# Where a tile is transposed in a two-layer recurrent trunk: matrix engine or vector engine

## The chip, the core and the metric

The kernel runs on one core of a Trainium2 chip. The core has five engines that run their own instruction streams in order: TensorE (PE) multiplies matrices, VectorE (DVE) and ScalarE (ACT) work elementwise, GpSimd (POOL) does a little elementwise work, and SyncE (SP) issues nearly all transfers between HBM and the on-chip memory SBUF. TensorE writes only to PSUM; the other engines read its results from there. The metric is the device time of one execution in microseconds (us), as the median of several runs.

## The reference

A causal decoder trunk of two layers over 512 positions with 2048 channels. Layer 0 joins a gated linear recurrence (RG-LRU) and a matrix LSTM (mLSTM) behind one input projection; layer 1 is a Mamba-2 SSD mixer in 8 groups of 8 heads. Cut to what the change touches:

```
def reference(x, ...):
    x = x + lru_mlstm_layer(rmsnorm(x, e_norm), ...)      # layer 0
    x = x + ssd_layer(rmsnorm(x, o_norm), ...)            # layer 1
    return rmsnorm(x, final_norm)

# layer 0, mLSTM half: per head, v feeds a causal attention with decays
v = einsum('bshi,hij->bshj', xm_h, w_v)
h = mlstm_chunkwise(q, k, v, ig, lf)

# layer 1
z, xbc, dt = split(x @ w_in)
xbc = silu(causal_conv(xbc, conv_w, conv_b))
xs, bm, cm = split(xbc)
da_cs  = cumsum(dt * a)                                   # inside chunks of 128 positions
decay  = exp(where(causal, da_t[l] - da_t[s], -inf))
cb     = einsum('bclgn,bcsgn->bcgls', cm, bm)
y_diag = einsum('bcgls,bcgels,bcsgep->bclgep', cb, decay, xdt)
states = einsum('bclgn,bclge,bclgep->bcgepn', bm, decay_states, xdt)
y      = y_diag + y_off(states) + d_skip * xs
y      = rmsnorm_grouped(y * silu(z)) @ w_out
```

All arrays are float32. Sums over positions (in `y_diag`, `states` and the mLSTM's attention) need `xs`, `bm` and `v` with positions on the partitions, while the projections leave them with channels on the partitions. That is why they are transposed.

## The kernel before

**Tiling.** Activations are tiles of 128 channels by 512 positions. To keep float32 accuracy at the fast matmul format, each operand is split into a high and a low part: `split` (L167 to L169) makes `hi` by a cast on ScalarE and `lo = src - hi` on VectorE. Each product is then three matmuls (`mm3`, L146 to L150: hi·hi, hi·lo, lo·hi). Weights stream from HBM all through the kernel: `load_w` (L129) reads 512 KB into one of two `wraw` buffers by a transfer on SyncE's queue and splits it into two pairs `whi`, `wlo` of 128 x 512, which rotate through four buffers each. `chunk` (L153) uses one such pair for 12 matmuls of 512 columns.

**Order of the work.** A tile framework plans the order of each engine's instructions from the order of the program, with priorities: `load_w` puts its transfer and its splits 3000 instructions ahead, as far as free buffers allow, and `evac` (the step that empties a PSUM bank on VectorE) 1000 ahead. Side work runs in generators: `spawn` starts one, `tick()` is called after nearly every chunk, and `yield n` in a generator means "go on n ticks from now". The table `LAG` (L43) holds these numbers. `tc.issue_after(ins)` orders what is issued inside it behind `ins` on the same engine.

**Layer 0.** For each of 4 heads the kernel projects `xm` and `zm`, then makes 4 tiles of v, 4 of o and 4 of q and k. For each v tile `vgen` (L403) waits 2 ticks, transposes the tile's four 128 x 128 blocks on TensorE into one PSUM bank, copies the bank to `vn` on ScalarE and sends it to HBM (`vd`), from where the attention reads it later.

**Layer 1.** Eight groups follow each other. For each group the kernel projects B and C (`xbc`: projection, evacuation with the norm factor, a causal convolution on ScalarE and VectorE, SiLU on ScalarE), then four tiles `xs` of two heads each, then four gate tiles `z`. Between the second and third tile of either four, some tiles of the previous group's output projection (`outproj`, PSUM tile `po`) are put in; the rest follow at the end. The generator `bcgen` (L748) makes C·B of each chunk (`CB`) and transposes three chunks of B on TensorE (`Btr`), which `split` then reads from PSUM into `Bn`. For each `xs` tile the generator `pair` (L768):

- fetches the two heads' decay sums, broadcast to all partitions (`dab`, two buffers), with a transfer on SyncE's queue;
- after 6 ticks transposes four chunks of `xs` on TensorE into PSUM (`xtr`), and VectorE multiplies that PSUM tile into `xw` (for the states) and `xdt` (for the diagonal part);
- for each head forms `min(dab - dasT, 0)` in four VectorE instructions of 128 x 128 (L798), takes `Exp` on ScalarE (L800) and multiplies by `CB` on VectorE (L801), giving `Pt`;
- after 4 more ticks runs the sixteen small matmuls `yd` and adds their result to `xs`.

The PSUM has three banks for projections (`pmm`) and four for side work (`pax`).

Of the kernel before, what the change touches and what calls it, by code (L numbers as in the profile page):

```python
# [9 lines left out]
F32 = mybir.dt.float32  # L10
F32R = mybir.dt.float32r
AF = mybir.ActivationFunctionType
# [4 lines left out]
P = 128  # L17
# [4 lines left out]
NH = 4  # L22
# [17 lines left out]

NRES = OFF["gsel"][0]

LAG = dict(P=6, rs=2, late=3, dtr=15, CB=5, xtr=6, st=4, sts=2, yo0=4, yo=2, att_rs=4, vtr=2, aitr=12, num=7, pr=2)  # L43

VB = (2, 2)

# [7 lines left out]
def trunk(ctx, tc, x_t, par, w_in0, w_qkvo, w_lru, w_if, w_out0, w_in1, w_out1, out):  # L54
# [68 lines left out]
        while gens:  # L123
            tick()

    last_hi = []


    def load_w(src, dsts=(None, None), ahead=3000):  # L129
        out = []  # L130
        with tc.high_priority(offset=ahead):
            n = src.shape[-1]
            raw = wp.tile([P, 1024], F32, tag="wraw", name="wraw", bufs=2)
            dma(raw[:, :n], src)
            for i in range(0, n, 512):
                m = min(512, n - i)
                if dsts[i // 512] is None:
                    hi = wp.tile([P, 512], F32R, tag="whi", name="whi", bufs=4)
                    lo = wp.tile([P, 512], F32R, tag="wlo", name="wlo", bufs=4)
                else:  # L140
                    hi, lo = dsts[i // 512]
                split(hi[:, :m], lo[:, :m], raw[:, i:i + m])
                out.append((hi, lo))
        return out

# [21 lines left out]
    def split(hi, lo, src):  # L167
        last_hi[:] = [sc.copy(hi, src)]  # L168
        return v.tensor_tensor(lo, src, hi.bitcast(F32), op=SUB)  # L169
# [4 lines left out]
    def axt(name="ax"):  # L174
        return pax.tile([P, S], F32, tag="ax", name=name)


    def recip(dst, src, w=S):
        for o in range(0, w, P):
            v.reciprocal(dst[:, o:o + P], src[:, o:o + P])  # L180

# [183 lines left out]
    for h in range(NH):  # L367
        xm, xc = [], []
        for t in range(4):
            j = 4 * h + t  # L370
            if h:
                ps = mmt("xm")
                proj(ps, w_in0[16 + j], xpairs)
            else:
                ps = ps01[j]
            raw = next_raw()
            evac(raw[:, 3:], ps, r_bc, MUL)
            m = xslot("xm")
            split(m[0], m[1], raw[:, 3:])
            xm.append(m)  # L380
            a = st("ca")
            conv(a, raw, pc("cm_w", 4 * j, 4), pc("cm_b", j))
            sc.activation(a, a, AF.Silu)
            c = xslot("xc")
            split(c[0], c[1], a)
            xc.append(c)
            tick()
            if j == 0:

                softplus(nlam, pc("lam", 0, 16), -1.0, *[st("ln")[:, :16] for _ in range(3)])  # L390
                v.tensor_scalar(nlam, nlam, -8.0, None, op0=MUL)
        zm = []
        for t in range(4):
            j = 4 * h + t
            ps = mmt("zm") if j else axt("zm")
            proj(ps, w_in0[48 + j], xpairs)
            z = PA.tile([P, S], F32, tag="zm", name="zm", bufs=4)
            evac(z, ps, r_bc, MUL)
            sc.activation(z, z, AF.Silu)
            zm.append(z)  # L400
            tick()

        def vgen(vt, h, t):  # L403
            yield LAG["vtr"]
            pt = axt("vtr")
            for s in range(4):
                pe.transpose(pt[:, s * P:(s + 1) * P], vt[:, s * P:(s + 1) * P], ident)
            vn = PA.tile([P, 4, P], F32, tag="vn", name="vn", bufs=2)
            sc.copy(vn.rearrange("p a b -> p (a b)"), pt)
            dma(vd[h][:, :, t * P:(t + 1) * P], vn)  # L410

        def ggen(kt, rhs):
            yield 2
            gate_mm(kt, rhs)

        vts = []
        for t in range(4):
            if t % 2 == 0:
                ws = load_w(w_qkvo[h, 2 + t // 2])
            ps = mmt("v")  # L420
            chunk(ps, ws[t % 2], xm, 0, 4)
            vt = PA.tile([P, S], F32, tag="vt", name="vt", bufs=5)
            sc.copy(vt, ps)
            vts.append(vt)
            spawn(vgen(vt, h, t))
            tick()
        spawn(ggen([16 + 4 * h + t for t in range(4)], vts))
        for t in range(4):
            if t % 2 == 0:
                ws = load_w(w_qkvo[h, 4 + t // 2])  # L430
            ps = mmt("o")
            chunk(ps, ws[t % 2], xm, 0, 4)
            s = st("os")
            sc.activation(s, ps, AF.Sigmoid)
            v.scalar_tensor_tensor(zm[t], zm[t], pc("m_norm", 4 * h + t), s, op0=MUL, op1=MUL)
            dma(od[h][t], zm[t])
            tick()
        qk = []
        for t in range(4):
            if t % 2 == 0:  # L440
                ws = load_w(w_qkvo[h, 0 + t // 2])
            ps = mmt("qk")
            chunk(ps, ws[t % 2], xc, 0, 4)
            q = PA.tile([P, S], F32, tag="qk", name="qk", bufs=4)
            if t < 2:
                sc.copy(q, ps)
                dma(qd[h][t], q)
            else:
                sc.activation(q, ps, AF.Copy, scale=1.0 / 16)
                dma(kd[h][t - 2], q)  # L450
            qk.append(q)
            tick()
        spawn(ggen([2 * h, 2 * h + 1, 8 + 2 * h, 9 + 2 * h], qk))
# [237 lines left out]
    def lt(tag, bufs=1, shape=(P, S), dt=F32):  # L691
        return L1.tile(list(shape), dt, tag=tag, name=tag, bufs=bufs)
# [55 lines left out]
    def bcgen(G):  # L748
        Bt, Ct = G["Bt"], G["Ct"]
        CB = lt("CB", shape=(P, 4, P))  # L750
        Bn = lt("Bnh", shape=(P, 3 * P), dt=F32R), lt("Bnl", shape=(P, 3 * P), dt=F32R)
        G["CB"], G["Bn"] = CB, Bn
        yield LAG["CB"]
        ps = axt("CB")
        for c in range(4):
            cs = slice(c * P, (c + 1) * P)
            pe.matmul(ps[:, cs], Bt[:, cs], Ct[:, cs], start=True, stop=True)
        v.tensor_tensor(CB, ps.rearrange("p (c l) -> p c l", l=P),
                        mask.unsqueeze(1).to_broadcast([P, 4, P]), op=MUL)
        ps = axt("Btr")  # L760
        for c in range(3):
            cs = slice(c * P, (c + 1) * P)
            pe.transpose(ps[:, cs], Bt[:, cs], ident)
        split(Bn[0], Bn[1], ps[:, :3 * P])
        G["bc"] = True


    def pair(G, t, xs):  # L768
        CB = G["CB"]
        j = 4 * G["g"] + t  # L770
        h0 = 2 * j
        pts = []
        dabs = []
        for e in range(2):
            dab = lt("dab", 2)
            dma(dab, dad[h0 + e].partition_broadcast(P))
            dabs.append(dab)
        yield LAG["xtr"]
        assert G["bc"] and len(ready) == 3
        ps = axt("xtr")  # L780
        for c in range(4):
            cs = slice(c * P, (c + 1) * P)
            pe.transpose(ps[:, cs], xs[:, cs], ident)
        p4 = ps.rearrange("p (c h d) -> p c h d", h=2, d=64)
        xdt = lt("xdt", 2, (P, 4, P))
        if t == 0:
            G["xw"] = lt("xw", 1, (P, 3, 4, P))
        xw = G["xw"][:, :, t].rearrange("p c (h d) -> p c h d", d=64)
        v.tensor_tensor(xw, p4[:, 0:3],
                        dwT[:, 0:3, h0:h0 + 2].unsqueeze(3).to_broadcast([P, 3, 2, 64]), op=MUL)  # L790
        v.tensor_tensor(xdt.rearrange("p c (h d) -> p c h d", d=64), p4,
                        dtT[:, :, h0:h0 + 2].unsqueeze(3).to_broadcast([P, 4, 2, 64]), op=MUL)
        if t == 3:
            spawn(states(G))
        for e in range(2):
            pt = lt("Pt", 2, (P, 4, P))
            for c in range(4):
                v.tensor_scalar(pt[:, c], dabs[e][:, c * P:(c + 1) * P], dasT[:, c, h0 + e:h0 + e + 1], 0.0,  # L798
                                op0=SUB, op1=MIN)
            sc.activation(pt, pt, AF.Exp)  # L800
            v.tensor_tensor(pt, pt, CB, op=MUL)  # L801
            pts.append(pt)
        yield LAG["st"]
        pd = axt("yd")
        for c in range(4):
            for e in range(2):
                pe.matmul(pd[e * 64:(e + 1) * 64, c * P:(c + 1) * P], xdt[:, c, e * 64:(e + 1) * 64],
                          pts[e][:, c], start=True, stop=True)
        v.scalar_tensor_tensor(xs, xs, pc("dskip", j), pd, op0=MUL, op1=ADD)
        G["yd"][t] = xs  # L810
# [332 lines left out]
```

## Time and profile before

| | |
|---|---|
| median of 3 runs | 2628.41 us (2628.21 to 2628.78) |
| the profiled execution, its own time | 2627.02 us |
| its span, first to last instruction | 2625.2 us |
| VectorE busy | 1670.0 us, 64% |
| ScalarE busy | 1214.5 us, 46% |
| transfers | 295 MB, 33.8% of the 16 DMA engines' time |

In the profile a line of a timeline gives start and duration in us, the engine (PE for a matmul, PEld for the weight load before it), the line of the code, the operation, `out<-in` by tile names, the shape and the count, and in brackets the idle time before it with what ended that. Matmuls overlap in their pipeline: the listed duration of one is its latency, and what it costs the stream is the distance from one start to the next. A row of `lines` gives a group's busy time and the mean duration of one; a row of `windows` the busy time (and the number of instructions) of PE, weight loads, VectorE, ScalarE and GpSimd in a stretch of time.

### The profile page before, as it was taken

The numbers are of one execution on the slowest core, as the hardware profiler recorded it, in microseconds if no ns is written. First come the engines' busy times: TensorE is split into PE (matmuls) and PEld (weight loads), VectorE is DVE, ScalarE is ACT, GpSimd is POOL, SyncE is SP. The second block draws the span as 40 slices with busy tenths as digits, with TensorE's granted clock in tenths as the row PEclk, the third lists the DMA queues.
The fourth block names the chain that finished last, engine by engine and source line by source line (L and its number), as shares of the span: only waits on it lengthen the run. The fifth ranks groups of instructions, "written<-read, shape, count | busy, mean of one in ns | idle before, by whom it ended". The sixth has DMA issues, their size and how long they took to land. (4 is left out here: it accounts for less than half of the span.)

```text
span 2625.2 us, 32843 instructions
## 1 busy us (share of the span) xinstructions
PE 2610.6 (99%) x12289; PEld 2149.0 (82%) x12289; DVE 1670.0 (64%) x2746; ACT 1214.5 (46%) x1895; POOL 118.2 (5%) x107
## 2 busy tenths in 40 slices
PE   9999999999999999999999999999999999999998
PEld 8887878788888888888888888888888888888887
DVE  8452534488757757765777666666666666666675
ACT  6443443476536446453554333443434434334444
POOL 1000000010000000000200000000000000000002
PEclk9999999999999999999999999999999999999999
DMA  5424242533333333332253332333333333233322
GB/s 185 135 98 144 93 141 96 159 105 129 115 107 112 115 103 104 106 109 97 87 130 109 104 117 97 115 105 105 108 104 113 102 104 117 93 118 107 105 98 105
DMA packets 113919, 295.09 MB, mean 112 GB/s; under 512 B 11992, under 2 KB 37336, under 8 KB 113760
## 3 DMA queue, kind: packets, MB, share of 16 engines
q1 hardware_dynamic: 113616, 292.73, 33.8%
q8 instruction: 97, 1.59, 0.2%
q14 instruction: 62, 0.51, 0.1%
q10 hardware_dynamic: 144, 0.26, 0.0%
HBM read 275.89 MB, written 17.06 MB: 112 GB/s over the span
## 5 line engine op out<-in xcount | busy, mean ns | idle before, releaser
L168 ACT CAST whi<-wraw 128x512 fp32r<-128x512 f32 (+1 forms) x881 | 541.3, 615 | 1026.4 <-PE po L149 276.0
L169 DVE TENSOR_TENSOR wlo<-wraw,whi 128x512 fp32r<-128x512 f32 (+1 forms) x881 | 622.9, 708 | 510.3 <-ACT whi L168 484.4
L148 PE MATMUL xbc<-xh,whi 128*128 128x512 f32 x768 | 301.1, 392 | 0.0
L150 PE MATMUL xbc<-xh,wlo 128*128 128x512 f32 x768 | 299.0, 389 | 0.0
L149 PE MATMUL xbc<-xl,whi 128*128 128x512 f32 x768 | 298.9, 389 | 0.0
L227 DVE TENSOR_TENSOR acc<-acc,po 128x512 f32<-128x512 f32 (+1 forms) x257 | 174.2, 680 | 178.7 <-PE po L150 178.2
L148 PE MATMUL z<-xh,whi 128*128 128x512 f32 x512 | 203.9, 398 | 0.0
L150 PE MATMUL z<-xh,wlo 128*128 128x512 f32 x512 | 199.8, 390 | 0.0
L149 PE MATMUL z<-xl,whi 128*128 128x512 f32 x512 | 199.3, 389 | 0.0
L148 PE MATMUL po<-yh,whi 128*128 128x512 f32 (+1 forms) x456 | 178.1, 390 | 0.0
L150 PE MATMUL po<-yh,wlo 128*128 128x512 f32 (+1 forms) x456 | 176.8, 388 | 0.0
L149 PE MATMUL po<-yl,whi 128*128 128x512 f32 (+1 forms) x456 | 176.6, 387 | 0.0
L148 PEld LDWEIGHTS xbc<-xh,whi 128*128 128x128 f32 x768 | 144.2, 188 | 30.5 <-issue 1.2
L150 PEld LDWEIGHTS xbc<-xh,wlo 128*128 128x128 f32 x768 | 144.1, 188 | 30.3
L149 PEld LDWEIGHTS xbc<-xl,whi 128*128 128x128 f32 x768 | 144.2, 188 | 29.4
L245 POOL TENSOR_TENSOR ssq<-ssq,sq 128x512 f32<-128x512 f32 x51 | 66.3, 1300 | 1571.4 <-ACT sq L244 1571.4
L150 PEld LDWEIGHTS z<-xh,wlo 128*128 128x128 f32 x512 | 96.1, 188 | 20.9
L149 PEld LDWEIGHTS z<-xl,whi 128*128 128x128 f32 x512 | 96.3, 188 | 18.8
L148 PEld LDWEIGHTS z<-xh,whi 128*128 128x128 f32 x512 | 96.2, 188 | 18.5
L148 PE MATMUL zl<-xh,whi 128*128 128x512 f32 x256 | 101.4, 396 | 0.0
L148 PE MATMUL po<-ylh,whi 128*128 128x512 f32 x256 | 100.7, 393 | 0.0
L150 PEld LDWEIGHTS po<-yh,wlo 128*128 128x128 f32 x456 | 85.6, 188 | 17.9
(372 smaller groups left out, 5311.2 us busy)
## 6 DMA issues: line engine op xcount, KB each, us to landing
wraw<-in_w_in_dram SPq DMA_DIRECT2D x287, 512.0 KB, 3.2
wraw<-in_w_out_dram SPq DMA_DIRECT2D x128, 512.0 KB, 3.2
dab<-dad SPq DMA_DIRECT2D x64, 256.0 KB, 3.2
wraw<-in_w_qkvo_dram SPq DMA_DIRECT2D x24, 512.0 KB, 3.2
E<-ed SPq DMA_DIRECT2D x64, 96.0 KB, 2.7
vd<-vn SPq DMA_DIRECT2D x16, 256.0 KB, 3.7
od<-zm SPq DMA_DIRECT2D x16, 256.0 KB, 3.8
V<-vd SPq DMA_DIRECT2D x16, 256.0 KB, 3.9
```

Of the source, the lines that this page charges most:

```text
L148: pe.matmul(ps, wh, mh, start=first, stop=False)
L149: pe.matmul(ps, wh, ml, start=False, stop=False)
L150: return pe.matmul(ps, wl, mh, start=False, stop=last)
L168: last_hi[:] = [sc.copy(hi, src)]
L169: return v.tensor_tensor(lo, src, hi.bitcast(F32), op=SUB)
L227: v.tensor_tensor(o, a, b, op=op)
L245: eng.tensor_tensor(ssq, ssq, sq, op=ADD)
```

## The change

- `flip` is new. It transposes on VectorE: for a tile of 128 partitions it issues, for each of four source quadrants `a` and four target quadrants `b`, one instruction that transposes the 32 x 32 blocks of `n` chunks, 16 instructions in all for a whole tile. Each reads 32 partitions by `n` x 32 elements from SBUF and writes as many to SBUF. All are ordered behind the last `lo` instruction of a weight split traced so far, which `last_lo` remembers.
- `vgen`: all v tiles but the last of the last head are flipped into `vn` in four parts of four instructions, one tick apart, starting after 2 + 3t ticks for tile t. The last one is done as before.
- `bcgen`: in groups 1 to 7, B is flipped into an SBUF tile from the `s` ring in two parts of eight instructions, one tick apart (`n` is 3), and split from there.
- `pair`: in groups 1 to 7, `xs` is flipped into `xdt` in two parts of eight instructions (`n` is 4) at ticks 4 and 5. At tick 6, as before, `xw` and then `xdt` itself, in place, are made from that tile in SBUF. Group 0 is transposed on TensorE as before.
- `min(dab - dasT, 0)` becomes `relu(dasT - dab)` on ScalarE, in as many instructions, in all eight groups, and the sign moves into the `Exp`.

```diff
-LAG = dict(P=6, ..., CB=5, xtr=6, st=4, ...)
+LAG = dict(P=6, ..., CB=5, flip=4, xtr=2, st=4, ...)

-                split(hi[:, :m], lo[:, :m], raw[:, i:i + m])
+                last_lo[:] = [split(hi[:, :m], lo[:, :m], raw[:, i:i + m])]

+    def flip(dst, src, lo, hi):
+        n = dst.shape[1]
+        s4 = src[:, :n * P].rearrange("p (c b i) -> p c b i", b=4, i=32)
+
+        with tc.issue_after(last_lo[0].ins):
+            for a in range(lo, hi):
+                pa = slice(32 * a, 32 * a + 32)
+                for b in range(4):
+                    v.transpose(dst[32 * b:32 * b + 32, :, pa], s4[pa, :, b])

         def vgen(vt, h, t):
-            yield LAG["vtr"]
-            pt = axt("vtr")
...
+            if h == NH - 1 and t == 3:
+                yield LAG["vtr"]
+                pt = axt("vtr")
...
+            else:
+
+                yield LAG["vtr"] + 3 * t
+                vn = PA.tile([P, 4, P], F32, tag="vn", name="vn", bufs=2)
+                for a in range(4):
+                    if a:
+                        yield 1
+                    flip(vn, vt, a, a + 1)
             dma(vd[h][:, :, t * P:(t + 1) * P], vn)

+        if G["g"] == 0:
...
+        else:
+            bt = st("bt")[:, :3 * P].rearrange("p (c n) -> p c n", n=P)
+            flip(bt, Bt, 0, 2)
+            yield 1
+            flip(bt, Bt, 2, 4)
+            split(Bn[0], Bn[1], bt.rearrange("p c n -> p (c n)"))

-        yield LAG["xtr"]
+        yield LAG["flip"]
+        xdt = lt("xdt", 2, (P, 4, P))
+        if G["g"]:
+            flip(xdt, xs, 0, 2)
+            yield LAG["xtr"] - 1
+            flip(xdt, xs, 2, 4)
+            yield 1
+            p4 = xdt.rearrange("p c (h d) -> p c h d", d=64)
+        else:
+
+            yield LAG["xtr"]
+            ps = axt("xtr")
...
             for c in range(4):
-                v.tensor_scalar(pt[:, c], dabs[e][:, c * P:(c + 1) * P], dasT[:, c, h0 + e:h0 + e + 1], 0.0,
-                                op0=SUB, op1=MIN)
-            sc.activation(pt, pt, AF.Exp)
+                sc.activation(pt[:, c], dabs[e][:, c * P:(c + 1) * P], AF.Relu, bias=dasT[:, c, h0 + e:h0 + e + 1],
+                              scale=-1.0)
+            sc.activation(pt, pt, AF.Exp, scale=-1.0)
```

More of the change, by code (lines that the diff above doesn't have):

```diff
@@ L41 @@
 NRES = OFF["gsel"][0]
-LAG = dict(P=6, rs=2, late=3, dtr=15, CB=5, xtr=6, st=4, sts=2, yo0=4, yo=2, att_rs=4, vtr=2, aitr=12, num=7, pr=2)
+LAG = dict(P=6, rs=2, late=3, dtr=15, CB=5, flip=4, xtr=2, st=4, sts=2, yo0=4, yo=2, att_rs=4, vtr=2, aitr=12, num=7, pr=2)
 VB = (2, 2)
@@ L124, in drain @@
             tick()
-    last_hi = []
+    last_hi, last_lo = [], []
     def load_w(src, dsts=(None, None), ahead=3000):
@@ L403, in vgen @@
         def vgen(vt, h, t):
-            yield LAG["vtr"]
-            pt = axt("vtr")
[L406 to L409, printed above, removed]
+            if h == NH - 1 and t == 3:
+                yield LAG["vtr"]
+                pt = axt("vtr")
+                for s in range(4):
+                    pe.transpose(pt[:, s * P:(s + 1) * P], vt[:, s * P:(s + 1) * P], ident)
+                vn = PA.tile([P, 4, P], F32, tag="vn", name="vn", bufs=2)
+                sc.copy(vn.rearrange("p a b -> p (a b)"), pt)
+            else:
+                yield LAG["vtr"] + 3 * t
+                vn = PA.tile([P, 4, P], F32, tag="vn", name="vn", bufs=2)
+                for a in range(4):
+                    if a:
+                        yield 1
+                    flip(vn, vt, a, a + 1)
             dma(vd[h][:, :, t * P:(t + 1) * P], vn)
@@ L759, in bcgen @@
                         mask.unsqueeze(1).to_broadcast([P, 4, P]), op=MUL)
[L760 to L764, printed above, removed]
+        if G["g"] == 0:
+            ps = axt("Btr")
+            for c in range(3):
+                cs = slice(c * P, (c + 1) * P)
+                pe.transpose(ps[:, cs], Bt[:, cs], ident)
+            split(Bn[0], Bn[1], ps[:, :3 * P])
+        else:
[4 more added lines that the diff above has]
+            split(Bn[0], Bn[1], bt.rearrange("p c n -> p (c n)"))
         G["bc"] = True
@@ L777, in pair @@
             dabs.append(dab)
-        yield LAG["xtr"]
-        assert G["bc"] and len(ready) == 3
[L780 to L785, printed above, removed]
+        yield LAG["flip"]
[9 more added lines that the diff above has]
+            ps = axt("xtr")
+            for c in range(4):
+                cs = slice(c * P, (c + 1) * P)
+                pe.transpose(ps[:, cs], xs[:, cs], ident)
+            p4 = ps.rearrange("p (c h d) -> p c h d", h=2, d=64)
+        assert G["bc"] and len(ready) == 3
         if t == 0:
```

## The prediction, written before the changed kernel was run

> **What bounds the kernel now.** I read the page first, then TensorE's own list of waits from 60 to 2500 us, then the busy time of one whole group of layer 1.
>
> ```profile
> span 2625.2 us, 32843 instructions
> ...
> PE 2610.6 (99%) x12289; PEld 2149.0 (82%) x12289; DVE 1670.0 (64%) x2746; ACT 1214.5 (46%) x1895; POOL 118.2 (5%) x107
> ```
> ```profile
> PE den L606 <- DVE M L191: 1.1, 1, 1.1
> ```
> ```profile
> 1602.20:1767.70 165.50, 165.50 (x799) 136.58 (x798) 109.00 (x187) 66.66 (x102) 3.88 (x3) 1.00 0.32 107
> ```
>
> A busy PE alone proves little, since matmuls overlap. The waits prove more: in 2440 us TensorE waits once, for 1.1 us. The window row shows PE busy in all 165.50 us of a group, VectorE in 109.00 and ScalarE in 66.66, at a granted clock of 1.00. So the time is the length of TensorE's stream. What leaves the stream is gained, as long as no other engine begins to hold it up. How far the others are ahead is read where they wait:
>
> ```profile
> 1653.13 0.62 ACT L168 CAST whi<-wraw 128x512 fp32r<-128x512 f32 x1 [2.09 <-PE xbc L149]
> ```
> ```profile
> 1651.07 0.69 DVE L169 TENSOR_TENSOR wlo<-wraw,whi 128x512 fp32r<-128x512 f32 x1 [1.22 <-ACT whi L168]
> 1653.78 0.69 DVE L169 TENSOR_TENSOR wlo<-wraw,whi 128x512 fp32r<-128x512 f32 x1 [2.02 <-ACT whi L168]
> ```
> ```profile
> 1623.22 0.69 DVE L227 TENSOR_TENSOR acc<-acc,po 128x512 f32<-128x512 f32 x1 [1.43 <-PE po L150]
> ...
> 1625.94 0.69 DVE L227 TENSOR_TENSOR acc<-acc,po 128x512 f32<-128x512 f32 x1 [1.43 <-PE po L150]
> ```
>
> One chunk of 12 matmuls takes 2.71 us (1651.07 to 1653.78), 0.226 us a matmul. The cast waits for PE to give back a weight buffer, and the subtraction for the cast. With four buffers, a pair that is finished 1.4 us after its buffer came free is used three chunks after that moment: **lead of the weights** 3 x 2.71 - 1.34 = 6.8 us. The evacuations of `po` also wait for PE; with three banks the next use of a bank starts two chunks later: **lead of the banks** 2 x 2.72 - 0.69 = 4.75 us. A delay on VectorE shorter than that costs nothing.
>
> **What TensorE loses.** The three groups of transposes, and their neighbours in its timeline:
>
> ```profile
> L783 PE MATMUL xtr<-prm,xs 128*128 128x128 f32 x128 | 20.1, 280 | 0.0
> L407 PE MATMUL vtr<-prm,vt 128*128 128x128 f32 x64 | 9.6, 272 | 0.0
> L763 PE MATMUL Btr<-prm,Bt 128*128 128x128 f32 x24 | 3.9, 272 | 0.0
> ```
> ```profile
> 98.37 0.39 PE L150 MATMUL v<-xmh,wlo 128*128 128x512 f32 x1
> 98.60 0.60 PE L407 MATMUL vtr<-prm,vt 128*128 128x128 f32 x4
> ...
> 99.27 0.39 PE L149 MATMUL v<-xml,whi 128*128 128x512 f32 x1
> ...
> 1464.09 0.66 PE L783 MATMUL xtr<-prm,xs 128*128 128x128 f32 x4
> ...
> 1464.82 0.39 PE L149 MATMUL po<-yl,whi 128*128 128x512 f32 x1
> ...
> 1602.21 1.05 PE L757 MATMUL CB<-Ct,Bt 128*128 128x128 f32 x8
> 1603.10 0.49 PE L763 MATMUL Btr<-prm,Bt 128*128 128x128 f32 x3
> ...
> 1603.66 0.40 PE L149 MATMUL xbc<-xl,whi 128*128 128x512 f32 x1
> ...
> 1616.85 0.40 PE L150 MATMUL po<-yh,wlo 128*128 128x512 f32 x1
> 1617.09 0.60 PE L783 MATMUL xtr<-prm,xs 128*128 128x128 f32 x4
> ...
> 1617.76 0.40 PE L149 MATMUL po<-yl,whi 128*128 128x512 f32 x1
> ...
> 1641.08 1.09 PE L807 MATMUL yd<-Pt,xdt 128*64 128x128 f32 x16
> 1642.10 0.50 PE L148 MATMUL xbc<-xh,whi 128*128 128x512 f32 x1
> 1642.44 0.40 PE L149 MATMUL xbc<-xl,whi 128*128 128x512 f32 x1
> ...
> 1767.69 1.05 PE L757 MATMUL CB<-Ct,Bt 128*128 128x128 f32 x8
> ```
>
> The latency of 0.27 us is not the price; the starts are. Between big matmuls (98.37 to 99.27, 1616.85 to 1617.76) the two starts around a group of four and one more matmul are 0.90 and 0.91 us apart, where two plain steps would be 0.45: **0.45 us** a group. Right behind the small `yd` matmuls, 0.73 us pass from the transposes to the second matmul after them (1464.09 to 1464.82); without transposes in between (1642.10 to 1642.44) it is 0.34, which the stream pays anyway: **0.39 us**. `Btr` always follows `CB`: 0.56 less the same 0.34, **0.22 us**. In groups 1 to 7 each group has two transposes of the first and two of the second kind (`CB` returns after 165.48 us, from 1602.21 to 1767.69, so the pattern repeats). Sum: v 15 x 0.45 = 6.8; x 14 x 0.45 + 14 x 0.39 = 11.8; B 7 x 0.22 = 1.5; together **20.1 us**. The ticks at which `xw`, `xdt` and `yd` come stay the same, so the rest of the stream keeps its order.
>
> **What VectorE gets.** It issues 28 x 16 + 15 x 16 + 7 x 16 = 800 transposing instructions and loses 256 bounds. No transpose ran on it before. The nearest rows:
>
> ```profile
> L798 DVE TENSOR_SCALAR Pt<-dab,dasT 128x128 f32<-128x128 f32 x256 | 55.4, 280 | 0.0
> L180 DVE RECIPROCAL ssq<-std 128x128 f32<-128x128 f32 x48 | 44.4, 939 | 9.2 <-ACT std L201 9.2
> L569 DVE TENSOR_TENSOR Pt<-Pt,S 128x128 f32<-128x128 f32 x4 | 1.1, 273 | 0.0
> L212 DVE TENSOR_TENSOR gG<-gG,g 4x512 f32<-4x512 f32 x6 | 4.0, 675 | 0.1
> L213 DVE TENSOR_SCALAR prm<-prm 128x16 f32<-128x16 f32 x6 | 1.0, 167 | 0.0
> L710 DVE TENSOR_TENSOR_SCAN xs<-ones_r,xs 128x128 f32<-128x128 f32 x2 | 0.7, 406 | 0.0
> ```
>
> Four partitions by 512 take 675 ns, and 128 by 512 took 0.69 us above, so the partitions don't count: a transpose of 32 partitions by 128 elements is bounded below by the 167 ns of 16 elements and above by the 939 ns of the slowest operation on 128. I take 0.28, that of plain operations on 128 elements, since a transpose passes each element once. That is 16 x 0.28 = 4.5 us per `xs` tile, for 0.4 us on TensorE.
>
> [...]
>
> Per group, VectorE has 109.0 - 32 x 0.216 (55.4 / 256) + 80 x 0.28 = 124.5 us in about 163.6: 76%. The tight place is where pairs 0 and 1 meet the output projection:
>
> ```profile
> 1613.20:1646.30 33.10, 33.10 (x172) 26.92 (x171) 22.60 (x47) 12.19 (x19) 0.00 (x0) 1.00 0.31 106
> ...
> 90.00:140.00 50.00, 50.00 (x235) 39.50 (x234) 15.11 (x22) 20.41 (x35) 0.00 (x0) 1.00 0.50 158
> ```
>
> There 22.60 - 16 x 0.216 + 32 x 0.28 = 28.1 us of 33.1: it fits. A block of eight is 2.2 us; what is queued behind it in VectorE's order is the next weight subtraction (lead 6.8 us) or an evacuation (lead 4.75 us), for which TensorE waits; both cover it. The v tiles add 64 x 0.28 = 17.9 us to the 15.11 of 50: hidden. So are the multiplications of `xw`, `xdt` and `Bn`, which read SBUF in place of PSUM at the same length.
>
> **What ScalarE gets.** 256 bounds with a per-partition bias; it loses 15 copies, which I leave out.
>
> ```profile
> L711 ACT ACTIVATE xs<-xs 128x128 f32<-128x128 f32 x2 | 0.8, 400 | 0.3 <-DVE xs L710 0.3
> ...
> L800 ACT ACT_TABLE_LOAD x19 | 24.4, 1283 | 4.5 <-DVE Pt L798 4.2
> ```
>
> The first row is the same form (bias per partition, scale -1, 128 x 128): 0.40 us. A group gets 32 x 0.40 = 12.8 us on 66.66: hidden. In a bad order a cast stands behind eight of them and a table load: 3.2 + 1.28 = 4.5 us, under 6.8. If each of 64 batches needed table loads of its own, a group would get 8 x 2 x 1.28 = 20.5 us more and still be at 61%.
>
> [...]
>
> **SyncE's queue.** Weight transfers stand behind `dab` and `vd` transfers there:
>
> ```profile
> SPq L66 <- DVE wlo L169: 1793.2, 424, 8.2
> SPq L66 <- DVE Pt L798: 166.7, 48, 7.0
> ...
> SPq L66 <- ACT vn L409: 25.6, 8, 3.9
> ```
>
> The queue already waits up to 7.0 us for a `dab` buffer without TensorE noticing. Now ScalarE frees it, independent of the transposes, and `vn` is freed by transposes paced over three ticks. I cost both at nothing; if the cover were gone, some us per head.
>
> **The rivals.**
>
> 1. *Part is given back.* If a transpose takes 0.41 us, as the scan's row, the tight window holds 19.1 + 13.1 = 32.3 of 33.1 us, and a block (3.3 us) next to three other instructions of 0.69 is 5.35 us, over the banks' lead by 0.6. Twice a group, seven groups: 8.4 us back, 2617. For it: VectorE's queue is in order. Against: 0.41 is half as much again as a plain operation.
> 2. *VectorE becomes the bound, slower than before.* In the tight window the stall per group is 19.1 + 32x - 33.1 - 4.75; it eats the gain (20.1 / 7 = 2.9) from x = 0.67 us on. At the reciprocal's 0.94 it is 11.3 us, 79 in seven groups, less 20: 2687. Nothing but the missing row speaks for it.
> 3. *Nothing is gained.* The transposes hide in some other limit, such as weight loads (82%) or transfers: 2628. Against it is every cast and subtraction that waits for PE, not for a transfer.
> 4. *More is gained.* If a group of transposes is worth its whole listed 0.60 us (0.49 for B): 43 x 0.60 + 7 x 0.49 = 29.2, time 2599.
>
> **How the numbers follow.** The sum stands against the profiled execution: span 2625.2 - 20.1 = 2605.1, its own time 2627.02 - 20.1 = 2606.9. The median of the runs is 1.4 us above that one: 2628.41 - 20.1 = **2608.3**. Chances: all hidden 0.66 (2605 to 2611); rival 1 0.14 (2612 to 2624); rival 2 0.09; rival 3 0.06; rival 4 0.05. A measurement can tell 0.2% (5.3 us) from no change: faster is below 2623.2. That makes faster 0.85, same 0.06, slower 0.09. The range 2602 to 2622 leaves out rivals 2 and 3 and the ends of 1 and 4.
>
> **What would show it.** Right: a group's period falls from 165.5 to about 163.6 us (2 x 0.45 + 2 x 0.39 + 0.22 = 1.9), TensorE's list of waits stays nearly empty, the transposes' mean is near 0.28 us, VectorE is at 76% in a group and ScalarE at about 49%, and casts still wait for PE. Wrong: a matmul that waits for VectorE or ScalarE in groups 1 to 7, or gaps above 0.23 us between starts near the blocks of eight; a mean above 0.4 us; table loads well above before's; or groups 1 to 7 of unequal length.

## The result and the profile after

The changed kernel takes **2612.42 us** in the median of six runs (2609.38 to 2615.89), the kernel before 2628.6 (2628.05 to 2629.97): a ratio of 0.9937, with a 95% interval of 0.9927 to 0.9948. It is 16.2 us faster; 20.1 were forecast. The profiled execution took 2611.91 us, its span is 2610.1. First two lines of the changed kernel's profile page, then TensorE's own list of waits between 60 and 2500 us, then a whole group of layer 1 (group 2; groups count from 0):

```profile
span 2610.1 us, 33167 instructions
...
PE 2590.5 (99%) x12096; PEld 2131.2 (82%) x12096; DVE 1856.4 (71%) x3290; ACT 1276.9 (49%) x2136; POOL 117.7 (5%) x107
```
```profile
PE yd L844 <- DVE xdt L828: 2.0, 1, 2.0
PE yd L844 <- DVE Pt L838: 1.3, 1, 1.3
PE den L627 <- DVE M L203: 0.9, 1, 0.9
PE pr L148 <- DVE Pt L590: 0.9, 1, 0.9
PE S L588 <- DMA k<-kd: 0.5, 1, 0.5
```
```profile
1599.75:1763.00 163.25, 163.25 (x780) 134.60 (x779) 125.90 (x236) 75.28 (x134) 3.88 (x3) 1.00 0.32 108
```

TensorE has 193 matmuls less and is still busy through a whole group of layer 1. VectorE rose from 109.00 to 125.90 us in it, ScalarE from 66.66 to 75.28. But there is a wait that was not there before: `yd` for `xdt` and for `Pt`, once each. The new operations, from the groups of instructions of VectorE and of ScalarE:

```profile
L192 DVE STREAM_TRANSPOSE xdt<-xs 32x128 f32<-32x128 f32 x448 | 135.7, 303 | 17.2 <-ACT xs L767 10.0
L192 DVE STREAM_TRANSPOSE vn<-vt 32x128 f32<-32x128 f32 x240 | 72.7, 303 | 3.9
L192 DVE STREAM_TRANSPOSE bt<-Bt 32x96 f32<-32x96 f32 x112 | 30.2, 269 | 1.8
```
```profile
L835 ACT ACTIVATE Pt<-dab,dasT 128x128 f32<-128x128 f32 x256 | 83.0, 391 | 18.3 <-PE yd L844 18.3
...
L837 ACT ACT_TABLE_LOAD x19 | 24.4, 1283 | 0.3
```

A transpose of 128 elements takes 303 ns (forecast 280), one of 96 elements 269. The ReLU takes 391 ns (forecast 400), and no table load was added: 19 as before.

Where the time went is read from one matmul group that occurs once per group of layer 1, `CB`. Its starts in TensorE's timeline, before (groups 0 and 1; the later ones stand in the prediction) and after (groups 0 to 4). A row ends where the stretch shown ends, so only its start counts here, not its length or its count:

```profile
1314.12 0.60 PE L757 MATMUL CB<-Ct,Bt 128*128 128x128 f32 x4
...
1436.72 0.49 PE L757 MATMUL CB<-Ct,Bt 128*128 128x128 f32 x3
```
```profile
1308.48 0.72 PE L778 MATMUL CB<-Ct,Bt 128*128 128x128 f32 x5
...
1431.08 0.60 PE L778 MATMUL CB<-Ct,Bt 128*128 128x128 f32 x4
...
1599.64 0.60 PE L778 MATMUL CB<-Ct,Bt 128*128 128x128 f32 x4
...
1763.00 0.49 PE L778 MATMUL CB<-Ct,Bt 128*128 128x128 f32 x3
...
1926.36 0.49 PE L778 MATMUL CB<-Ct,Bt 128*128 128x128 f32 x3
```

Layer 0 gave 1314.12 - 1308.48 = 5.6 us. Group 0 is unchanged (122.6). Groups 2 to 6 take 163.36 in place of 165.49: 2.13 us each. **Group 1 takes 168.56 in place of 165.49: it lost 3.1 us** where it should have gained 2.1. That is the shortfall.

### The profile page after: what moved, and what is told of

The parts are those of the page before. It is cut to its first block, busy times and chain, and to the rows that moved or that the text cites. A ratio compares the mean times of both kernels' runs of the same rounds, so it can differ in the third digit from the quotient of the medians.

```text
span 2610.1 us, 33167 instructions
## 1 busy us (share of the span) xinstructions
PE 2590.5 (99%) x12096; PEld 2131.2 (82%) x12096; DVE 1856.4 (71%) x3290; ACT 1276.9 (49%) x2136; POOL 117.7 (5%) x107
## 3 DMA queue, kind: packets, MB, share of 16 engines
q8 instruction: 95, 1.56, 0.2%
## 5 line engine op out<-in xcount | busy, mean ns | idle before, releaser
L192 DVE STREAM_TRANSPOSE xdt<-xs 32x128 f32<-32x128 f32 x448 | 135.7, 303 | 17.2 <-ACT xs L767 10.0
L148 PEld LDWEIGHTS po<-yh,whi 128*128 128x128 f32 x456 | 85.8, 188 | 18.6 <-issue 1.2
```

The lines of the kernel that those rows point to most:

```text
L148: pe.matmul(ps, wh, mh, start=first, stop=False)
L192: v.transpose(dst[32 * b:32 * b + 32, :, pa], s4[pa, :, b])
```

## What happened in group 1

TensorE's and VectorE's timelines of the changed kernel there:

```profile
1456.24 0.39 PE L150 MATMUL po<-yh,wlo 128*128 128x512 f32 x1
1458.61 0.40 PE L844 MATMUL yd<-Pt,xdt 128*64 128x128 f32 x2 [1.98 <-DVE xdt L828]
1460.32 1.97 PE L844 MATMUL yd<-Pt,xdt 128*64 128x128 f32 x14 [1.31 <-DVE Pt L838]
1462.22 0.80 PE L148 MATMUL po<-yh,whi 128*128 128x512 f32 x1
1462.82 0.63 PE L149 MATMUL po<-yl,whi 128*128 128x512 f32 x1
```
```profile
1453.27 2.21 DVE L192 STREAM_TRANSPOSE xdt<-xs 32x128 f32<-32x128 f32 x7
...
1457.18 0.68 DVE L838 TENSOR_TENSOR Pt<-Pt,CB 128x512 f32<-128x512 f32 x1
1457.79 0.68 DVE L828 TENSOR_TENSOR xdt<-xdt,dtT 128x512 f32<-128x512 f32 x1
```

The last seven transposes of group 1's first x tile end at 1455.5, `xdt` is ready at 1458.47, and the `yd` matmuls have been at the head of TensorE's queue since 1456.6. After the wait the next two big matmuls start 0.60 us apart; right behind `yd` 0.34 is usual (1642.10 to 1642.44 in the prediction's rows). TensorE's granted clock there is 0.50:

```profile
1460.00:1463.20 3.20, 2.88 (x16) 2.40 (x17) 3.08 (x9) 1.28 (x5) 0.00 (x0) 0.50 0.51 164
```

So of the 5.2 us that group 1 takes more than group 2, 3.3 are waits, and the other 1.9 are for the most part the slow stretch behind them.

The windows of the same place, two stretches of group 1 and the same two of group 2, in the kernel **before**:

```profile
1415.00:1436.70 21.70, 21.70 (x97) 17.98 (x96) 17.22 (x24) 12.52 (x19) 1.29 (x1) 1.00 0.32 106
1436.70:1458.00 21.30, 21.30 (x103) 17.76 (x102) 18.36 (x31) 9.74 (x16) 0.00 (x0) 1.00 0.24 84
```
```profile
1580.50:1602.20 21.70, 21.70 (x97) 17.97 (x96) 11.51 (x17) 9.02 (x13) 0.00 (x0) 1.00 0.30 97
1602.20:1623.50 21.30, 21.30 (x103) 17.78 (x102) 14.72 (x24) 8.08 (x13) 0.00 (x0) 1.00 0.25 81
```

In group 2 VectorE had 26.2 of 43 us there, in group 1 35.6. The difference is the end of group 0. Groups 1 to 6 close with six tiles of output projection, during which their last normalisation runs; group 0 has no earlier group to project, so its normalisation (reciprocals, scaling, splits) falls on group 1's B and first x tile. The first scaling of group 0 starts 1.9 us before group 1's `CB`, that of group 1 27.7 us before group 2's:

```profile
1434.83 0.75 DVE L879 SCALAR_TENSOR_TENSOR xs<-xs,prm,ssq 128x512 f32<-128x512 f32 x1
...
1574.51 0.75 DVE L879 SCALAR_TENSOR_TENSOR xs<-xs,prm,ssq 128x512 f32<-128x512 f32 x1
```

The change adds 16 x 0.27 + 16 x 0.30 = 9.1 us: 44.7 in 43, which does not fit. The bounds that leave VectorE don't help here, since none ran in that stretch (before, group 1's first eight start at 1382.72, the next at 1466.10). What does not fit comes later. In the changed kernel VectorE is busy for 40.09 of the 41 us up to the end of the wait; the same stretch of the kernel before, 5.64 us later by `CB` of group 1, has 33.80:

```profile
1420.00:1461.00 41.00, 37.71 (x174) 31.02 (x174) 40.09 (x82) 18.34 (x28) 0.00 (x0) 0.99 0.25 80
```
```profile
1425.64:1466.64 41.00, 41.00 (x202) 33.90 (x201) 33.80 (x55) 18.74 (x28) 0.00 (x0) 1.00 0.26 90
```

So the tight place stands in the trace of before, one group earlier than the one that the prediction looked at.

**Theory A**: TensorE's stream shrank as worked out, and only the place in group 1 gives some back. **Rivals**: the loss comes from elsewhere (the ReLUs' move, the shift of layer 0, whichever group is flipped first), or margin is thin everywhere.

## The experiments

The times below stand beside their own runs of the kernel before (2628.45 to 2628.84).

### The parts by themselves

`e1_relu_only` keeps every transpose on TensorE and moves only the bound; `e2_v_only` moves only the v tiles; `e3_layer1_only` moves all but the v tiles.

```diff
 e1: -        if G["g"]:                      # x, and B and v likewise
     +        if False:
 e2: as e1 for x and B, the four v.tensor_scalar back in place of the ReLU
 e3: -            if h == NH - 1 and t == 3:
     +            if True:
```

> Only the bound as a ReLU on ScalarE; all transposes stay on TensorE. Theory A (TensorE's stream is the time; ScalarE and VectorE have room): 2628.6 us within 1.5, a group's period 165.5, VectorE's busy time down by some 55 us and ScalarE's up by some 83. Rival (the move itself shortens or lengthens the path, since VectorE waits less or casts wait behind eight ReLUs): 5 us or more away from 2628.6, with TensorE waits in a group.

> Only the v tiles are transposed on VectorE; x, B and the bound as before. Theory A: four heads give 1.9, 1.9, 1.9 and 1.45 us, so 2628.6 - 7.2 = 2621.4. If the 1.6 us that were lost near 635 us in layer 0 of the changed kernel come from TensorE being ahead of the attention's loads, and not from layer 1, they are lost here too: 2623. Rival (that loss is chance of one execution): no wait near 635 us and 2621.

> x and B on VectorE in groups 1 to 7 and the bound on ScalarE; v on TensorE as before. Theory A: 7 x 2.13 = 14.9 us leave TensorE's stream and about 5.2 come back as the stall in group 1 (TensorE waits 2.0 us for xdt and 1.3 for Pt, then runs at a lower granted clock): 2628.6 - 9.7 = 2618.9, group 1 at 168 to 169 us, groups 2 to 6 at 163.3. Rival (the stall in group 1 follows from the earlier layer's shift): group 1 at 163.4 and 2614.

Measured: e1 **2630.05** us, ratio 1.0005 (0.9995 to 1.0014); e2 **2622.0**, 0.9972 (0.9961 to 0.9983); e3 **2620.24**, 0.9963 (0.9949 to 0.9977).

The ReLU alone changes nothing that can be measured; its groups keep 165.49 us, though VectorE drops by 47 us:

```profile
PE 2611.4 (99%) x12289; PEld 2149.8 (82%) x12289; DVE 1622.8 (62%) x2490; ACT 1289.2 (49%) x2151; POOL 117.6 (4%) x107
```

e3 has the stall of group 1 with the same two waits, though nothing of layer 0 moved, so the shift of layer 0 is not its cause. Its `CB` starts in groups 1, 2 and 3, and the window behind the stall:

```profile
1437.46 0.38 PE L778 MATMUL CB<-Ct,Bt 128*128 128x128 f32 x2
...
1607.44 0.38 PE L778 MATMUL CB<-Ct,Bt 128*128 128x128 f32 x2
...
1770.80 0.38 PE L778 MATMUL CB<-Ct,Bt 128*128 128x128 f32 x2
```
```profile
1467.00:1473.00 6.00, 6.00 (x25) 4.77 (x22) 5.70 (x17) 3.48 (x7) 0.00 (x0) 0.52 0.40 131
```

Group 1 takes 169.98 here, group 2 163.36. After the same 3.3 us of waiting, TensorE's granted clock is 0.52 over the next 6 us, and big matmuls start 0.43 us apart. In the changed kernel's profile the big matmuls were back at 0.23 after 1.3 us.

A second loss of the changed kernel lies in layer 0: 15 v tiles at 0.48 us are 7.2, and it gave 5.6. The 1.6 us are lost near 635 us, where `S` waits 0.5 us and `pr` 0.9. The wait of `pr` is there in e2 (1.7 us), but also in e1, whose layer 0 is that of the kernel before:

```profile
PE pr L148 <- DVE Pt L590: 1.2, 1, 1.2
```

In e1 VectorE waits 2.8 us for the transfer `M<-md` just before. So this loss differs from one execution to the next and isn't the change's; the expectation that e2 would tell was wrong, e1 did.

### Group 1's place

`e4_group1_on_pe` leaves group 1 on TensorE, `e8_one_pair_on_pe` only its first x tile, and `e9_early_norm` moves nothing between engines but starts group 0's normalisation two ticks earlier.

```diff
 e4: -        if G["g"]:                                   # and B's condition: G["g"] < 2
     +        if G["g"] > 1:
 e8: -        if G["g"]:
     +        if G["g"] > 1 or G["g"] == 1 and t:
 e9: -        yield LAG["late"] if G["g"] < NG - 1 else 1
     +        yield 1 if G["g"] in (0, NG - 1) else LAG["late"]
```

> As the changed kernel, but group 1 too is transposed on TensorE. Theory A (group 1 stalls because group 0's last normalisation falls on VectorE into the same 20 us as group 1's B and first x tile): no stall at all, group 1 at 165.5, group 2 at 163.3; against the changed kernel's 2612.4 it loses 2.1 us of gain and wins back 5.2: 2609.3. Rival (the first group that is flipped pays, whichever it is): group 2 at about 168.5 and 2614.5.

> As the changed kernel, but of group 1 only the first x tile is transposed on TensorE (0.45 us); its other three tiles and its B stay on VectorE. Theory A (the first x tile of group 1 is what comes too late, since its sixteen transposes stand behind group 0's last normalisation): no wait of yd, group 1 at 163.8, 2607.9 - 1.7 = 2606.2. Rival (B's sixteen transposes already fill that place, so that the next thing in it is late): yd still waits for Pt or xdt in group 1 and the time lies between 2608 and 2612.

> As the changed kernel, but group 0's normalisation chain starts 2 ticks (5.4 us) earlier after its last gate tile. Nothing is moved between engines. Theory A (VectorE has this chain, B and the first x tile of group 1 in one row without idle time, and the row starts too late): the row starts earlier, yd waits for under 1 us, 2606 to 2609. Rival (only the number of transposes counts, not when the chain runs): yd waits 3.3 us as in the changed kernel, 2612.

Measured: e4 **2607.91** us, ratio 0.9919 (0.9904 to 0.9933); e8 **2607.61** (2606.63 to 2608.82), 0.992 (0.9905 to 0.9934); e9 **2608.9**, 0.9922 (0.9905 to 0.9938). In all three `yd` waits no more. `CB` of groups 1 and 2 in e8:

```profile
1431.25 0.49 PE L778 MATMUL CB<-Ct,Bt 128*128 128x128 f32 x3
...
1595.07 0.49 PE L778 MATMUL CB<-Ct,Bt 128*128 128x128 f32 x3
```

163.82 us, as theory A has it; in e4 group 1 takes 165.48 and group 2 163.37, so it is not "the first flipped group, whichever it is". e9 shows that the place in time is the cause: the same work, begun 5 us earlier, no longer makes `yd` late. It pays 1.9 us over groups 0 and 1 together (287.88 in place of 122.60 + 163.36). TensorE is idle for 0.8 of these, 0.56 of it in one wait of `CB`, the only one in its list there; the rest is not placed:

```profile
PE CB L778 <- ACT Ct L767: 0.6, 1, 0.6
```

For e8 2606.2 was expected, for e4 2609.3; as measured the two can't be told apart. Every run of e8 is below every run of the changed kernel, so this one line is worth some 4 to 5 us.

### The bound back on VectorE

```diff
-                sc.activation(pt[:, c], dabs[e][...], AF.Relu, bias=dasT[...], scale=-1.0)
-            sc.activation(pt, pt, AF.Exp, scale=-1.0)
+                v.tensor_scalar(pt[:, c], dabs[e][...], dasT[...], 0.0, op0=SUB, op1=MIN)
+            sc.activation(pt, pt, AF.Exp)
```

> All transposes as in the changed kernel, the bound back on VectorE. Theory A (only group 1 lacks room): the eight bounds of a tile, 1.7 us, add to VectorE where it is already full: group 1 at 168.7 + 1.7 to 3.5, groups 2 to 6 unchanged at 163.36, time 2614 to 2616. Rival (the ReLU's move is what makes the room in all groups): every group longer by 1 us or more, 2619 or more.

Measured: **2614.96** us, ratio 0.9945 (0.9929 to 0.9962). Groups 2 to 6 stay at 163.36, group 1 takes 170.51. Its two waits are as long as the changed kernel's, 2.0 and 1.3 us; the difference of group 1 is a longer stretch at 0.43 us a matmul behind them. So the time is as expected but not by the expected mechanism, and the ReLU's move gains nothing that these runs can tell: 2614.96 lies inside the changed kernel's runs.

### The whole of TensorE's share

`e6_no_transposes` leaves out every transpose, on both engines and in group 0 too, and reads the untransposed tiles:

```diff
-            flip(xdt, xs, 0, 2)
...
+            p4 = xs.rearrange("p (c h d) -> p c h d", h=2, d=64)
```

> Leaves out every transpose of x, V and B, on either engine and in group 0 too: what follows reads the untransposed tiles. It gives the whole of TensorE's share. Theory A: v 7.7, groups 1 to 7 14.9, group 0 1.8, together 24.4: 2628.8 - 24.4 = 2604.4, no stall, groups at 163.36. Rival (the listed 0.60 us of a group of four is its price): 48 x 0.60 + 8 x 0.49 = 32.7, so 2596.

Measured: **2604.91** us, ratio 0.9909 (0.9895 to 0.9924). TensorE's transposes were worth 23.8 us in all (expected 24.4), not the 32.7 of their listed durations. The changed kernel keeps 2.6 of it on TensorE by choice (group 0 takes 122.60 against 120.52 here, and one v tile 0.48), so without a stall it would be at some 2607.5, and e8, with 0.45 us more on TensorE, is there (2607.61).

### What a transpose may cost

The transposing instructions issued again, all of them (`e7`), one in four (`e10`), half (`e11`):

```diff
-                for b in range(4):
+                for b in (0, 1, 2, 3, 0):              # e10; e11: ..., 0, 1; e7: each of the four twice
```

> Every transposing instruction on VectorE is issued twice, so that a tile costs twice 16 x 0.30 us. By the prediction's rival 2 (the lead of the banks, 4.75 us, is what decides) the tight window holds 19.1 + 32 x 0.606 = 38.5 us of 37.85: 0.65 us a group, 10 us more in group 1, 2626. Theory B (the deadline is yd, four ticks after the tile; the second tile of a group has some 8 us there and gets 9.7 us more in front of it): 2 to 4 us in each of groups 2 to 7 and 10 in group 1, 2635 to 2650, and the waits listed are those of yd for xdt or Pt, not of a projection for a bank.

> One in four transposing instructions issued twice: 0.38 us in place of 0.30 a step, 6 us more on VectorE per group. Theory A (groups 2 to 7 have some us of margin before yd's deadline): groups 2 to 6 stay at 163.4 to 165, group 1 gets 3 to 5 us longer, 2615 to 2630. Rival (no margin: every further us on VectorE lands on TensorE, as the 24.2 us per group of the doubled kernel suggest): 169.4 a group, 2612 + 7 x 6 = 2654 and more.

> Half of the transposing instructions issued twice: 0.45 us a step, 12 us more per group. Theory A (margin): 168 to 172 a group, some 2640 to 2680. Rival (no margin): 175.5 a group, 2697 and more.

| | per step of four | time, us | groups 2 to 6, us |
|---|---|---|---|
| changed kernel | 4 x 0.30 | 2612.42 | 163.36 |
| e10 | 5 x 0.30 | 2617.89 | 163.36 |
| e11 | 6 x 0.30 | 2689.07 | 172 to 174 |
| e7 | 8 x 0.30 | 2808.36 | 187.5 to 187.7 |

`CB` of groups 2 and 3 in e10, and its largest wait of TensorE; then TensorE's longest waits and group 2's window in e11; then the waits in e7:

```profile
1604.13 0.49 PE L778 MATMUL CB<-Ct,Bt 128*128 128x128 f32 x3
...
1767.49 0.38 PE L778 MATMUL CB<-Ct,Bt 128*128 128x128 f32 x2
```
```profile
PE yd L844 <- DVE xdt L828: 4.2, 1, 4.2
```
```profile
PE st L148 <- ACT xwh L168: 27.1, 7, 4.2
PE yd L844 <- DVE xdt L828: 6.8, 2, 5.2
PE po L148 <- DVE acc L239: 3.9, 6, 0.8
```
```profile
1617.70:1791.20 173.50, 168.00 (x780) 136.57 (x779) 137.47 (x276) 74.59 (x134) 3.88 (x3) 0.98 0.31 102
```
```profile
PE yd L844 <- DVE xdt L828: 47.3, 19, 6.4
PE st L148 <- ACT xwh L168: 45.4, 7, 7.8
PE po L148 <- DVE raw L239: 20.5, 6, 3.4
```

A quarter more (6 us per group on VectorE) costs groups 2 to 6 nothing and of these groups makes only group 1 later (171.91); half more costs 10 us in each of them. The threshold lies between 0.38 and 0.45 us for what now takes 0.30. It is not reached because VectorE is full over the group: in e11 it works 137.47 of 173.50 us. It is reached because one tile is late: once per group the states' matmul `st`, two ticks behind the group's last x tile, waits some 4 us for the cast of `xw`, which waits for that tile's transposes (in group 2 they end at 1694.70, `xw` at 1696.54, the cast at 1697.20, and `st` starts at 1697.25). VectorE is busy for 18.97 of the 20 us up to there (1677 to 1697). Not all of the 10.1 us in group 2 are waits: PE is idle for 5.5, and a granted clock of 0.98 over the window explains some 3.5 of the rest. All expectations for e7 were far too low, those of both theories.

## Why the prediction was right, and where it was not

- **TensorE's stream is the time, and the start distances are its price.** Right. e6 gives 23.8 us for all transposes, where the prediction's prices give 22.4 and the corrected ones 24.4. The forecast's own 20.1 was small by a tenth: v cost 1.9 us a head (0.48 a tile, not 0.45) and a group 2.13 us (not 1.90), so 22 in all. Half of a group's difference is B: behind `CB` the next big matmul now comes 0.80 us after `CB`'s start (1599.64 to 1600.44) in place of 0.89 + 0.24 (1602.21 to 1603.34), so 0.33 us went, not 0.22. The step that charged the same 0.34 to `CB` as to `yd` was mis-sized: 0.23 was due there.
- **One group stands for all seven.** This step failed. "The pattern repeats" holds for TensorE's stream, but group 1's VectorE has group 0's normalisation in it, and the tight window was taken from group 2. It cost 5.2 us (168.56 against 163.36) and is most of the gap between 22 and 16; e4, e8 and e9 each remove it. Two of the prediction's own signs of being wrong are this one place: a matmul that waits for VectorE, and groups of unequal length.
- **The forecast's number.** 2612.42 lies just outside what the prediction gave 0.66 to, all hidden (2605 to 2611), and inside its range. That it is only 4.1 us from the forecast is in part luck: a sum that was 2 us too small met a stall of 5 us that was not in it.
- **The price of a transpose.** 0.28 was taken, 0.303 measured: near. The leads of 6.8 and 4.75 us were not what ran out first: in layer 1 of the changed kernel only `yd` waits, for the tile's own deadline in ticks, and in group 2 of e11 `st` waits 3.7 us, while matmuls that need a bank wait 1.3 (0.56 and 0.75). So rival 2's price was far too high: slower than before begins between 0.38 and 0.45 us for a transpose, where the prediction had 0.67. The forecast held with less margin than it claimed: more than a quarter and less than a half, not a factor of two.
- **A block behind weight casts, the queue of SyncE, the tables.** Right as far as seen: between 60 and 2500 us no big matmul of the changed kernel waits for a cast, a split or a bank (the PSUM banks, which VectorE and ScalarE empty here).
- **ScalarE takes the bound for nothing.** Right (e1), and it was also worth nothing that can be measured (e5). Its price was too high: ScalarE's busy time rose by 8.6 us a group, where 12.8 was charged: the sum took the listed 0.40 for each ReLU, but in a row they start 0.30 us apart (five take 1.58 us). The bound on VectorE in its place (e5) took 2.5 us more by the medians of e5 and the changed kernel, within their spread.
- **Rival 1, part given back,** came to pass in size, with 4 us less gained than forecast, but in another place and by another mechanism: a tile that is late, once, not banks twice in each group.
- **The trade itself.** Right for this kernel: 238.6 us of transposes on VectorE replaced some 22 us on TensorE, and the time fell by 16.2 us. e11 shows how near it is to being wrong: with half of the transposes issued again it is 2689.07 us, where the kernel before takes 2628.45.

## What to carry to other kernels

When one engine's stream is the whole time, price an instruction on it by the distance of starts, and moving it to an engine with idle time can pay even at ten times the price, as it did here. But check the cover at each occurrence, the first one above all, since the work around it may differ there; and look for the deadline of the moved result itself (which matmul reads it, how many ticks later), not only for buffers and for the engine's share of busy time. Once a stream is freed, make it a test to issue the moved work one and a quarter times: it shows how far the edge is.

## What the hardware showed

- **A short wait of TensorE can cost more than itself.** Behind 3.3 us of waiting (1.98 and 1.31 us, with two small matmuls between them), matmuls of 512 columns started 0.60, 0.42 and 0.31 us apart instead of 0.226 in the changed kernel's profile, 1.3 us in all (granted clock 0.50 from 1460.0 to 1463.2). In e3 the granted clock was 0.52 over 6 us behind the same wait. In e11, behind the waits of `st` in groups 2 to 6 (3.7 to 4.2 us), the starts were 0.42 to 0.43 us apart from the third step on, and 0.23 again 6.4 us after the end of the wait in group 2 (1697.25 to 1703.61), 3.4 us after it in group 4 (2044.98 to 2048.36); behind a wait of `yd` of 1.56 us (to 1485.13) big matmuls were 0.34 and then 0.23 us apart. So the slow stretch is at about half the rate and differs in length; what sets its length no run here shows. The mean clock of a whole run goes with its span in the six runs of the changed kernel: 0.998 at 2607.5 us, 0.997 at 2609.8 to 2611.1, 0.996 at 2612.5 and 2613.9. That the slow stretch makes this spread is likely, not shown, since only one execution of each kernel has a trace.
- **The transposes here don't overlap each other.** Seven in a row take 2.21 us in the timeline above: a start every 0.32 us at a listed 0.303. Eight bounds in a row took 1.65 us before (at 1330.66): a start every 0.20 us at a listed 280 ns. Why the two differ no run here shows.
